# Hybrid decoder layer on one core: gathered operands for the level products, value projection of four heads at once

## The chip, the cores and the metric

The kernel runs on one core of one Trainium2 chip. The metric is the device time of one execution in microseconds (us). "PE" is TensorE, "DVE" VectorE, "ACT" ScalarE, "POOL" GpSimd, "SP" SyncE, which issues most DMAs; "PEld" is TensorE's loading of weights (the stationary operand). A matmul here multiplies a stationary tile of up to 128 x 128 with a moving tile of up to 512 columns into PSUM.

## The reference

One layer over 2048 tokens of width 1024, all in float32. The part that the change touches is the HGRN2 head group (4 heads, key and value width 128):

```python
proj = rmsnorm(h, norm_mix_w) @ w_in          # split into hq, hf, hi, hg and the attention columns
f = lb + (1 - lb) * sigmoid(hf); log_f = log(f); k = 1 - f; q = hq * 128 ** -0.5; v = hi
# per head:  S_t = diag(f_t) S_{t-1} + k_t v_t^T,   o_t = S_t^T q_t
o = rmsnorm(o, hg_norm_w) * silu(hg)
mix = concat([o, sliding_window_attention(...)])  # 8 query heads of 64, window 128, sink logits
h = h + mix @ w_out
h = h + (silu(causal_conv3(v @ w_gate)) * (v @ w_up)) @ w_down   # v = rmsnorm(h); d_ff = 2816
out = rmsnorm(h)
```

Inside a tile of 128 tokens the scores are sums of q_t k_s times the product of the f between s and t. For the kernel's purpose that is a triangle that can be built level by level.

## The kernel before, in words

The sequence is cut into two halves of 1024 tokens (`HALF`), each 8 tiles of 128 (`TT`). Activations lie transposed: features on the partitions, tokens along the free dimension. For each half the program runs a mixing stage (`hgrn`, `attend`, `project_v`), then `out_proj`, `gate_up` and `down`. Projections split each float32 operand into a high and a low part in a matmul format and use three matmuls (high x high, high x low, low x high); a projection of 128 columns is a `unit` of 48 matmuls with 512 moving columns. A weight comes as a 512 KB load into one of 3 `raw` buffers; `prep` (L185) casts its high part on ACT and subtracts it on DVE into one of 2 `hi` and one of 2 `lo` buffers, or, with `slots=True`, into two of the 8 buffers "m" of `slot`. A float32 matmul without such a split is two instructions on PE, and each counts as one in the profile.

Head by head (`HG` = 4) the mixing stage interleaves the generators `hgrn` and `attend`; a scheduler then orders each engine's queue by program order and a simulated timeline, so that independent matmuls (the units q, g, f, hq and, in the last head, `pop` of `out_proj`) are placed between dependent steps. In `hgrn`:

- f and hq are projected (L522, L527); K = 1 - f and Q = q f (L533 to L536) are two tiles with one buffer each.
- the diagonal of the score tile `ST` is a product of K and q (L544).
- seven levels m = 1, 2, 4, ... 64 follow (L590). In a level the tokens form blocks of m; every second block of Q meets the block of K before it. PE writes these products into `plev`. Then every second block of Q (L609) and the other blocks of K (L610) are multiplied with running products F of f, on DVE, in 512 elements each, and F itself is halved (L616, L620). In heads 0 to 2 and m < 32 the K blocks of two tiles are first gathered by ACT into `KK` (L566), so that one stationary tile serves two tiles of tokens (L569, 4 products); the results of the first tile are put into `ST` by a masked copy on DVE (L585), those of the second, which land on the wrong partitions, are copied to `moved` by ACT (L576), shifted by a DMA that ACT's queue issues (`odd`, L579), and placed by a second masked copy one level later (L588). In head 3, which runs beside `out_proj`, there is no gathering: 8 products a level (L602) and one masked copy of 512 elements (L625). m = 32 and m = 64 have 16 and 8 small products (L607), whose results ACT copies (L630).
- K is transposed on PE (`pkn`, L640), multiplied with v (`pu`, L647), and the state is run through the tiles on DVE (`SS`, L651).
- the outputs `po` (L665, L666) are 8 tiles in two PSUM banks; after each tile's products ACT squares them with a sum (L667). rsqrt on DVE, a scaling (`on`, L674), a transpose (`pot`, L679) and a product with the gate (L680) end the head.

`project_v` (L688) computes v for two heads at a time, 8 token tiles x 8 input tiles x 3 matmuls of 256 columns, in heads 0 and 2, with two prepared weights. `BEHIND` (L38) puts pieces of the first `pop` units behind the matmuls of head 3: unit 1 behind level 1, unit 2 in three parts behind `pu`, `po` and `pot`.

```python
elif h % 2 == 0:                                               # L1206
    next(at)
    wv = [prep(a["w_v"][h // 2, s]) for s in range(2)]
    next(hg)
    vs += project_v(hf, wv, X, rs, p)
```

Of the kernel before, what the change touches and what calls it, by code (L numbers as in the profile page):

```python
# [39 lines left out]
NEG = -1.0e30  # L40
UT = 7
RAW = 3
VB = 2
KB = 2
WARM = 12
TAIL_WARM = 7
LV = 4
# [3 lines left out]
def hymba_layer(ctx: ExitStack, tc: tile.TileContext, a: dict, out: bass.AP):  # L51
# [18 lines left out]
    def ps(kind, name):  # L70
        return spaces[kind].tile([P, 512], F32, tag=kind, name=name)
# [448 lines left out]
    def hgrn(hf, h, X, invb, vs, WG, mix, p, fu=None):  # L520
# [13 lines left out]
        nc.vector.tensor_scalar(K, f, -1.0, 1.0, op0=ALU.mult, op1=ALU.add)  # L534
        Q = p.tile([P, HALF], F32, tag="Q", name="Q", bufs=1)
        nc.vector.tensor_tensor(Q, q, f, op=ALU.mult)  # L536


# [19 lines left out]
            yield  # L558

        F, left = f, None  # L560

        def pairs():


            KK = p.tile([P, HALF // 2], F32, tag="KK", name="KK", bufs=KB)
            nc.scalar.copy(KK.rearrange("p (r b c m) -> p r c b m", r=TT // 2, c=2, m=m),  # L566
                           K.rearrange("p (r c b w m) -> p r c b w m", c=2, b=nbc, w=2, m=m)[:, :, :, :, 0])
            for r in range(TT // 2):
                marks[m] = nc.tensor.matmul(pl[:, r * P:(r + 1) * P], KK[:, r * P:(r + 1) * P],  # L569
                                            Qv[:, 2 * r * nbc:2 * (r + 1) * nbc, 1], start=True, stop=True)  # L570

        def place_pairs():

            plv = pl.rearrange("p (r c t) -> p r c t", r=TT // 2, c=2)
            moved, odd = [p.tile([P, TT // 2, 64], F32, tag="lv", name=n, bufs=LV) for n in ("moved", "odd")]
            nc.scalar.copy(moved, plv[:, :, 1])  # L576
# [5 lines left out]
            STv = ST.rearrange("p (r c) (b w m) -> p r c b w m", c=2, w=2, m=m)  # L582
            mk = C.lmask[m].bitcast(U32).rearrange("p (b m) -> p b m", m=m)
            mk = mk.unsqueeze(1).to_broadcast([P, TT // 2, nbc, m])
            nc.vector.copy_predicated(STv[:, :, 0, :, 1], mk, plv[:, :, 0].rearrange("p r (b m) -> p r b m", m=m))  # L585
            r = slice(0, P - m)
            ov = odd[r].rearrange("p r (b m) -> p r b m", m=m)
            return lambda: nc.vector.copy_predicated(STv[r, :, 1, :, 1], mk[r], ov)  # L588

        for m in LEVELS:  # L590
            nb = HALF // (2 * m)
            nbc = 64 // m
            Qv = Q.rearrange("p (b w m) -> p b w m", w=2, m=m)
            Kv = K.rearrange("p (b w m) -> p b w m", w=2, m=m)
# [3 lines left out]
            if paired:  # L598
                pairs()
            elif m < 32:  # L600
                for c in range(TT):
                    marks[m] = nc.tensor.matmul(pl[:, c * 64:(c + 1) * 64], K[:, c * P:(c + 1) * P],  # L602
                                                Qv[:, c * nbc:(c + 1) * nbc, 1], start=True, stop=True)
            else:
                for c in range(TT):
                    for s0 in range(0, P, 2 * m):
                        nc.tensor.matmul(pl[s0:s0 + m, c * m:(c + 1) * m], K[:, c * P + s0:c * P + s0 + m],  # L607
                                         Q[:, c * P + s0 + m:c * P + s0 + 2 * m], start=True, stop=True)
            nc.vector.tensor_tensor(Qv[:, :, 1], Qv[:, :, 1], Fv[:, :, 0:1].to_broadcast([P, nb, m]), op=ALU.mult)  # L609
            done = nc.vector.tensor_tensor(Kv[:, :, 0], Kv[:, :, 0], Fv[:, :, 1:2].to_broadcast([P, nb, m]), op=ALU.mult)  # L610
# [10 lines left out]
            if paired:  # L621
                left = place_pairs()
            elif m < 32:
                mk = C.lmask[m].bitcast(U32).rearrange("p (b m) -> p b m", m=m)
                nc.vector.copy_predicated(ST.rearrange("p c (b w m) -> p c b w m", w=2, m=m)[:, :, :, 1],  # L625
                                          mk.unsqueeze(1).to_broadcast([P, TT, nbc, m]),
                                          pl.rearrange("p (c b m) -> p c b m", c=TT, m=m))
            else:
# [32 lines left out]
        for c in range(TT):  # L661
            cs = slice(c * P, (c + 1) * P)
            prev = state[:, h] if c == 0 else SS[:, c - 1]
            o = po[c // 4][:, c % 4 * P:(c % 4 + 1) * P]
            nc.tensor.matmul(o, ST[:, c], v[:, c], start=True, stop=False)  # L665
            marks["po"] = nc.tensor.matmul(o, Q[:, cs], prev, start=False, stop=True)  # L666
            nc.scalar.activation(on[:, c], o, AF.Square, accum_out=ss[:, c:c + 1])  # L667
        rs = rsqrt(ss, TT, 1.0 / P)
        if h == HG - 1:
            mix[h] = new_x()  # L670
# [16 lines left out]

    def project_v(hf, parts, X, rs, p):  # L688

        v = [p.tile([P, TT, P], F32, tag="v", name="v", bufs=VB) for _ in range(2)]  # L690
        for tt in range(TT):
            o = ps("mm", "pvv")
            t = slice(tt * P, (tt + 1) * P)
            for kt in range(KT):
                hi, lo = parts[kt // 4]
                xh, xl = X[kt]
                c = slice((kt % 4) * 256, (kt % 4 + 1) * 256)
                nc.tensor.matmul(o[:, 0:256], xh[:, t], hi[:, c], start=kt == 0, stop=False)  # L698
                nc.tensor.matmul(o[:, 0:256], xl[:, t], hi[:, c], start=False, stop=False)  # L699
                nc.tensor.matmul(o[:, 0:256], xh[:, t], lo[:, c], start=False, stop=kt == KT - 1)  # L700
            for i in range(2):
                nc.scalar.activation(v[i][:, tt], o[:, i * P:(i + 1) * P], AF.Identity, scale=rs[:, tt:tt + 1])
        return v

    def split_into(h, l, src, eng=None):
        return (nc.scalar.copy(h, src),  # L706
# [480 lines left out]
    for hf in range(NH):  # L1187
        X, kv, invb, rs, f0 = nxt
        with ExitStack() as st:
# [45 lines left out]
def _layout(i):  # L1235
# [17 lines left out]
    w_v = np.stack([cols(w_in, 1024 + pr * 256 + ar(256)).reshape(P, 2, D).transpose(1, 0, 2) for pr in range(2)])  # L1253
    conv = np.concatenate([i["conv_w"][0], i["conv_b"]], 0)
    d = {
        "xT": x.T.reshape(KT, P, S),
# [37 lines left out]
```

## Time and profile before

| what | value |
|---|---|
| time, median of 3 runs | 2198.23 us (2197.66 to 2200.65) |
| span of the profiled execution | 2198.0 us |
| granted TensorE clock | 0.997 |
| PE, DVE, ACT busy | 2180.4, 1639.5, 1049.9 us |
| first half's mixing stage | about 45 to 397 us |
| second half's mixing stage | about 1137 to 1487 us |

The span is that of the first to the last instruction of one execution on the chip, read by its profiler. No other time of that execution is on record; the span lies 0.2 us under the median of the timed runs. A group's row gives line, engine, operation, result<-operands, shapes, count | busy time, mean ns of one | idle time of the engine before it and what ended that. Matmuls overlap in their pipeline, so the time from one start to the next says more than one's duration. Stretches of the first half's mixing stage: head 0 from 45, head 1 from 155, head 2 from 248, head 3 from 342 to 397 us.

### The profile page before, as it was taken

The numbers are of one execution on the slowest core, as the hardware profiler recorded it, in microseconds if no ns is written. First come the engines' busy times: TensorE is split into PE (matmuls) and PEld (weight loads), VectorE is DVE, ScalarE is ACT, GpSimd is POOL, SyncE is SP. The second block draws the span as 40 slices with busy tenths as digits, with TensorE's granted clock in tenths as the row PEclk, the third lists the DMA queues.
The fourth block names the chain that finished last, engine by engine and source line by source line (L and its number), as shares of the span: only waits on it lengthen the run. The fifth ranks groups of instructions, "written<-read, shape, count | busy, mean of one in ns | idle before, by whom it ended". The sixth has DMA issues, their size and how long they took to land.

```text
span 2198.0 us, 29524 instructions
## 1 busy us (share of the span) xinstructions
PE 2180.4 (99%) x11424; PEld 1834.0 (83%) x11424; DVE 1639.5 (75%) x2451; ACT 1049.9 (48%) x1848; POOL 6.3 (0%) x28
## 2 busy tenths in 40 slices
PE   9999999999999999999999999999999999999998
PEld 7988988888888888888889889888888888888888
DVE  6567568688887888885855666677888878887766
ACT  6445544454444445335735455544644444443353
POOL 1000000000000000000000000000000000000000
PEclk9999999999999999999999999999999999999999
DMA  4101112323333234964631111114132323259643
GB/s 155 51 32 48 39 41 68 119 74 102 104 109 108 89 127 143 372 241 156 209 125 41 44 36 51 58 39 134 58 125 92 125 91 109 98 183 393 233 144 130
DMA packets 94358, 257.91 MB, mean 117 GB/s; under 512 B 11594, under 2 KB 17546, under 8 KB 94218
## 3 DMA queue, kind: packets, MB, share of 16 engines
q1 hardware_dynamic: 88992, 251.30, 33.9%
q10 hardware_dynamic: 5226, 4.73, 0.7%
q8 instruction: 89, 1.46, 0.3%
q14 instruction: 51, 0.42, 0.1%
HBM read 195.10 MB, written 57.15 MB: 115 GB/s over the span
## 4 chain that ended last, share of the span: by engine, by line
PE 95%; DVE 3%; ACT 1%; DMA 1%; issue 0%; SPq 0%; DVEq 0%; ACTq 0%
PE X L877 7%; PE X L878 7%; PE X L879 7%; PE pop L212 7%; PE hq L212 4%; PE q L212 4%; PE f L212 4%; PE g L212 4%; PE Y L879 4%; PE Y L878 4%; PE Y L877 4%; PE pdx L1088 3%; PE pdx L1089 3%; PE pdx L1090 3%; PE pdy L1089 3%; PE pdy L1088 3%
## 5 line engine op out<-in xcount | busy, mean ns | idle before, releaser
L706 ACT CAST whi<-raw 128x1024 fp32r<-128x1024 f32 x88 | 92.6, 1053 | 109.2 <-PE X L878 68.2
L877 PE MATMUL X<-T,whi 128*128 128x512 f32 x352 | 136.9, 389 | 0.0
L878 PE MATMUL X<-T,whi 128*128 128x512 f32 x352 | 136.9, 389 | 0.0
L879 PE MATMUL X<-T,wlo 128*128 128x512 f32 x352 | 136.9, 389 | 0.0
L972 DVE SCALAR_TENSOR_TENSOR y<-ga,cw,y 128x1024 f32<-128x1024 f32 x88 | 112.5, 1281 | 26.0 <-ACT y L970 26.0
L884 ACT COPY u<-X 128x512 f32<-128x512 f32 x88 | 51.4, 585 | 133.3 <-PE X L879 133.1
L707 DVE TENSOR_TENSOR wlo<-raw,whi 128x1024 fp32r<-128x1024 f32 x88 | 107.3, 1220 | 0.0
L190 ACT CAST whi<-raw 128x1024 fp32r<-128x1024 f32 x57 | 59.5, 1048 | 93.1 <-PE q L212 31.9
L707 DVE TENSOR_TENSOR xld<-raw,xhd 128x1024 fp32r<-128x1024 f32 x72 | 80.8, 1133 | 19.1 <-ACT xhd L706 18.9
L706 ACT CAST xhd<-raw 128x1024 fp32r<-128x1024 f32 x72 | 69.7, 978 | 43.6 <-DMA raw<-act0T 14.8
L212 PE MATMUL pop<-XL,whi 128*128 128x512 f32 x256 | 86.1, 396 | 2.1 <-DVE XL L224 2.1
L212 PE MATMUL pop<-XH,wlo 128*128 128x512 f32 x256 | 85.2, 393 | 0.8 <-DVE wlo L191 0.8
L212 PE MATMUL pop<-XH,whi 128*128 128x512 f32 x256 | 84.5, 397 | 0.2
L878 PEld LDWEIGHTS X<-T,whi 128*128 128x128 f32 x352 | 66.1, 188 | 13.7
L877 PEld LDWEIGHTS X<-T,whi 128*128 128x128 f32 x352 | 66.1, 188 | 13.7
L879 PEld LDWEIGHTS X<-T,wlo 128*128 128x128 f32 x352 | 66.1, 188 | 13.7
L1088 PE MATMUL pdx<-xhd,hid 128*128 128x512 f32 x192 | 74.4, 391 | 1.0 <-ACT hid L706 1.0
L1089 PE MATMUL pdx<-xld,hid 128*128 128x512 f32 x192 | 74.7, 389 | 0.0
L1090 PE MATMUL pdx<-xhd,lod 128*128 128x512 f32 x192 | 73.7, 389 | 0.0
L698 PE MATMUL pvv<-whi,XH 128*128 128x256 f32 x256 | 73.5, 288 | 0.0
L191 DVE TENSOR_TENSOR wlo<-raw,whi 128x1024 fp32r<-128x1024 f32 x57 | 69.5, 1222 | 4.2 <-ACT whi L190 4.1
L699 PE MATMUL pvv<-whi,XL 128*128 128x256 f32 x256 | 72.6, 284 | 0.0
(379 smaller groups left out, 6563.3 us busy)
## 6 DMA issues: line engine op xcount, KB each, us to landing
wr<-in_w_down SPq DMA_DIRECT2D x90, 512.0 KB, 4.8
raw<-in_w_gate SPq DMA_DIRECT2D x44, 512.0 KB, 3.6
raw<-in_w_up SPq DMA_DIRECT2D x44, 512.0 KB, 3.6
raw<-act0T SPq DMA_DIRECT2D x20, 512.0 KB, 6.1
raw<-act1T SPq DMA_DIRECT2D x20, 512.0 KB, 10.1
act0B<-y SPq DMA_DIRECT2D x33, 256.0 KB, 2.6
act1B<-y SPq DMA_DIRECT2D x33, 256.0 KB, 2.4
raw<-in_w_out SPq DMA_DIRECT2D x16, 512.0 KB, 4.7
```

What stands on the lines that cost most here:

```text
L212: marks["unit"] = nc.tensor.matmul(o[b], w, x[:, bs], start=f, stop=l)
L698: nc.tensor.matmul(o[:, 0:256], xh[:, t], hi[:, c], start=kt == 0, stop=False)
L699: nc.tensor.matmul(o[:, 0:256], xl[:, t], hi[:, c], start=False, stop=False)
L706: return (nc.scalar.copy(h, src), (eng or nc.vector).tensor_tensor(l, src, h.bitcast(F32), op=ALU.subtract))
L707: (eng or nc.vector).tensor_tensor(l, src, h.bitcast(F32), op=ALU.subtract))
L877: nc.tensor.matmul(o, wh[:, ws], xh, start=i == 0 and not more, stop=False, skip_group_check=more)
L878: nc.tensor.matmul(o, wh[:, ws], xl, start=False, stop=False, skip_group_check=more)
L879: r = nc.tensor.matmul(o, wl[:, ws], xh, start=False, stop=i == 3, skip_group_check=more)
L972: nc.vector.scalar_tensor_tensor(y, g[:, w:w + HALF], C.cw[:, ft, w:w + 1], y, op0=ALU.mult, op1=ALU.add)
L1088: nc.tensor.matmul(o, wh[:, i, c], ah[:, i, cols], start=f, stop=False, skip_group_check=more)
L1089: nc.tensor.matmul(o, wh[:, i, c], al[:, i, cols], start=False, stop=False, skip_group_check=more)
L1090: nc.tensor.matmul(o, wl[:, i, c], ah[:, i, cols], start=False, stop=l, skip_group_check=more)
```

## The change

In `hgrn`, Q and K become the two halves of one tile `QK`. Every level, in every head, begins with one copy on ACT that gathers the blocks of both Q and K that the products read into a tile `G` (2 buffers, 1024 elements a partition), pairing tile r with tile r + 4. The products read `G`: 4 products of 128 x 128 for m < 32 in all heads and for m = 64, 16 small ones for m = 32. One DVE multiplication of 1024 elements updates Q and K together, in place of L609 and L610. Head 3 places its results like the others, with `moved`, `odd` and two masked copies of 256 elements. At m = 64 ACT copies the result in two pieces. The squares of `po` are issued behind all 16 products, in a loop of their own. `project_v` runs once in each half, in head 0, for all four heads, with 512 moving columns and four prepared weights, two of them in the slots "m"; one eviction of 512 elements a token tile takes the place of two of 128. Head 2 then takes the path of head 1. The scratch for dynamic DMA descriptors is set to 256.

```diff
-VB = 2
-KB = 2
+GB = 2
@@ hgrn
-        K = p.tile([P, HALF], F32, tag="K", name="K", bufs=1)
+        QK = p.tile([P, 2, HALF], F32, tag="QK", name="QK", bufs=1)
+        Q, K = QK[:, 0], QK[:, 1]
         nc.vector.tensor_scalar(K, f, -1.0, 1.0, op0=ALU.mult, op1=ALU.add)
-        Q = p.tile([P, HALF], F32, tag="Q", name="Q", bufs=1)
         nc.vector.tensor_tensor(Q, q, f, op=ALU.mult)
...
+        R = TT // 2
+        def place(m, pl):
+            plv = pl.rearrange("p (r b c m) -> p r b c m", r=R, c=2, m=m)
+            moved, odd = [p.tile([P, R, 64], F32, tag="lv", name=n, bufs=LV) for n in ("moved", "odd")]
+            nc.scalar.copy(moved.rearrange("p r (b m) -> p r b m", m=m), plv[:, :, :, 1])
             rows_ = P - max(m, 2)
             nc.scalar.dma_start(odd[0:rows_], moved[m:m + rows_])
...
+            nc.vector.copy_predicated(STv[:, 0, :, :, 1], mk, plv[:, :, :, 0])
...
+            return lambda: nc.vector.copy_predicated(STv[r, 1, :, :, 1], mk[r], ov)
         for m in LEVELS:
...
+            part, step = QK.ap[0], QK.ap[-1][0]
+            own = bass.AP(QK.tensor, QK.offset + m * step, [part, [(HALF - m) * step, 2], [2 * m * step, nb], [step, m]])
+            far = bass.AP(QK.tensor, QK.offset + m * step, [part, [(HALF - m) * step, 2], [2 * m * step, nb // 2],
+                                                           [R * P * step, 2], [step, m]])
+            G = p.tile([P, 2, HALF // 2], F32, tag="G", name="G", bufs=GB)
+            nc.scalar.copy(G.rearrange("p t (b c m) -> p t b c m", c=2, m=m), far)
             pl = ps("hg", "plev")
-            paired = m < 32 and h < HG - 1
...
+            if m == 32:
                 for c in range(TT):
+                    for b in range(2):
+                        x = slice(c % R * P + b * 64 + c // R * m, c % R * P + b * 64 + c // R * m + m)
+                        nc.tensor.matmul(pl[2 * b * m:2 * b * m + m, c * m:(c + 1) * m], G[:, 1, x], G[:, 0, x],
+                                         start=True, stop=True)
             else:
...
+                for r in range(R):
+                    x = slice(r * P, (r + 1) * P)
+                    marks[m] = nc.tensor.matmul(pl[:, x], G[:, 1, x], G[:, 0, x], start=True, stop=True)
-            nc.vector.tensor_tensor(Qv[:, :, 1], Qv[:, :, 1], Fv[:, :, 0:1].to_broadcast([P, nb, m]), op=ALU.mult)
-            done = nc.vector.tensor_tensor(Kv[:, :, 0], Kv[:, :, 0], Fv[:, :, 1:2].to_broadcast([P, nb, m]), op=ALU.mult)
+            done = nc.vector.tensor_tensor(own, own, Fv.rearrange("p b w -> p w b").unsqueeze(3).to_broadcast([P, 2, nb, m]),
+                                           op=ALU.mult)
...
+            if m < 32:
+                left = place(m, pl)
+            elif m == 32:
                 for s0 in range(0, P, 2 * m):
                     nc.scalar.copy(ST[s0:s0 + m, :, s0 + m:s0 + 2 * m], ...)
+            else:
+                for c in range(2):
+                    nc.scalar.copy(ST[0:m, c * R:(c + 1) * R, m:],
+                                   pl[c * m:(c + 1) * m].rearrange("p (r c m) -> p r c m", c=2, m=m)[:, :, c])
...
             marks["po"] = nc.tensor.matmul(o, Q[:, cs], prev, start=False, stop=True)
-            nc.scalar.activation(on[:, c], o, AF.Square, accum_out=ss[:, c:c + 1])
+        for c in range(TT):
+            nc.scalar.activation(on[:, c], po[c // 4][:, c % 4 * P:(c % 4 + 1) * P], AF.Square,
+                                 accum_out=ss[:, c:c + 1])
@@ project_v
-        v = [p.tile([P, TT, P], F32, tag="v", name="v", bufs=VB) for _ in range(2)]
+        v = p.tile([P, HG, TT, P], F32, name="v")
...
-                hi, lo = parts[kt // 4]
+                hi, lo = parts[kt // 2]
-                c = slice((kt % 4) * 256, (kt % 4 + 1) * 256)
-                nc.tensor.matmul(o[:, 0:256], xh[:, t], hi[:, c], start=kt == 0, stop=False)
+                c = slice((kt % 2) * 512, (kt % 2 + 1) * 512)
+                nc.tensor.matmul(o, xh[:, t], hi[:, c], start=kt == 0, stop=False)
...
-            for i in range(2):
-                nc.scalar.activation(v[i][:, tt], o[:, i * P:(i + 1) * P], AF.Identity, scale=rs[:, tt:tt + 1])
+            nc.scalar.activation(v[:, :, tt], o.rearrange("p (h d) -> p h d", h=HG), AF.Identity,
+                                 scale=rs[:, tt:tt + 1])
@@ mixing stage
-                elif h % 2 == 0:
+                elif h == 0:
                     next(at)
-                    wv = [prep(a["w_v"][h // 2, s]) for s in range(2)]
+                    wv = [prep(a["w_v"][s], s > 1) for s in range(4)]
                     next(hg)
                     vs += project_v(hf, wv, X, rs, p)
@@ kernel
-    nc = bacc.Bacc("TRN2", target_bir_lowering=False, num_devices=1)
+    nc = bacc.Bacc("TRN2", target_bir_lowering=False, num_devices=1, dynamic_dma_scratch_size=256)
```

More of the change, by code (lines that the diff above doesn't have):

```diff
@@ L560, in hgrn @@
         F, left = f, None
[L562 to L576, printed above, removed]
+        R = TT // 2
[3 more added lines that the diff above has]
+            nc.scalar.copy(moved.rearrange("p r (b m) -> p r b m", m=m), plv[:, :, :, 1])
             rows_ = P - max(m, 2)
@@ L581, in place_pairs @@
                 nc.scalar.dma_start(odd[rows_:rows_ + 1], moved[P - 1:P])
[L582 removed]
+            STv = ST.rearrange("p (c r) (b w m) -> p c r b w m", c=2, w=2, m=m)
             mk = C.lmask[m].bitcast(U32).rearrange("p (b m) -> p b m", m=m)
[L584 to L585 removed]
+            mk = mk.unsqueeze(1).to_broadcast([P, R, 64 // m, m])
+            nc.vector.copy_predicated(STv[:, 0, :, :, 1], mk, plv[:, :, :, 0])
             r = slice(0, P - m)
             ov = odd[r].rearrange("p r (b m) -> p r b m", m=m)
[L588 removed]
+            return lambda: nc.vector.copy_predicated(STv[r, 1, :, :, 1], mk[r], ov)
         for m in LEVELS:
@@ L596, in hgrn @@
+            G = p.tile([P, 2, HALF // 2], F32, tag="G", name="G", bufs=GB)
+            nc.scalar.copy(G.rearrange("p t (b c m) -> p t b c m", c=2, m=m), far)
             pl = ps("hg", "plev")
-            paired = m < 32 and h < HG - 1
-            if paired:
-                pairs()
-            elif m < 32:
+            if m == 32:
                 for c in range(TT):
-                    marks[m] = nc.tensor.matmul(pl[:, c * 64:(c + 1) * 64], K[:, c * P:(c + 1) * P],
-                                                Qv[:, c * nbc:(c + 1) * nbc, 1], start=True, stop=True)
-            else:
[L605 to L608, printed above, removed]
@@ L620, in hgrn @@
                 nc.vector.tensor_tensor(F, Fv[:, :, 0], Fv[:, :, 1], op=ALU.mult)
[L621 to L628, printed above, removed]
+            if m < 32:
+                left = place(m, pl)
+            elif m == 32:
                 for s0 in range(0, P, 2 * m):
@@ L694, in project_v @@
             for kt in range(KT):
-                hi, lo = parts[kt // 4]
+                hi, lo = parts[kt // 2]
                 xh, xl = X[kt]
-                c = slice((kt % 4) * 256, (kt % 4 + 1) * 256)
-                nc.tensor.matmul(o[:, 0:256], xh[:, t], hi[:, c], start=kt == 0, stop=False)
-                nc.tensor.matmul(o[:, 0:256], xl[:, t], hi[:, c], start=False, stop=False)
-                nc.tensor.matmul(o[:, 0:256], xh[:, t], lo[:, c], start=False, stop=kt == KT - 1)
-            for i in range(2):
-                nc.scalar.activation(v[i][:, tt], o[:, i * P:(i + 1) * P], AF.Identity, scale=rs[:, tt:tt + 1])
-        return v
+                c = slice((kt % 2) * 512, (kt % 2 + 1) * 512)
+                nc.tensor.matmul(o, xh[:, t], hi[:, c], start=kt == 0, stop=False)
+                nc.tensor.matmul(o, xl[:, t], hi[:, c], start=False, stop=False)
+                nc.tensor.matmul(o, xh[:, t], lo[:, c], start=False, stop=kt == KT - 1)
+            nc.scalar.activation(v[:, :, tt], o.rearrange("p (h d) -> p h d", h=HG), AF.Identity,
+                                 scale=rs[:, tt:tt + 1])
+        return [v[:, h] for h in range(HG)]
     def split_into(h, l, src, eng=None):
@@ L1252, in _layout @@
     w_out = i["w_out"][0][np.concatenate(rows)]
-    w_v = np.stack([cols(w_in, 1024 + pr * 256 + ar(256)).reshape(P, 2, D).transpose(1, 0, 2) for pr in range(2)])
+    w_v = cols(w_in, 1024 + ar(512)).reshape(P, 4, D).transpose(1, 0, 2)
     conv = np.concatenate([i["conv_w"][0], i["conv_b"]], 0)
```

2 lines of the change are left out of this document (removed).

## The prediction

> **What bounds the kernel now.** I read the page's busy shares first, then the chain that ended last by engine, then the stretches of the mixing stage, then the timeline of PE inside it.
>
> ```profile
> span 2198.0 us, 29524 instructions
> PE 2180.4 (99%) x11424; PEld 1834.0 (83%) x11424; DVE 1639.5 (75%) x2451; ACT 1049.9 (48%) x1848; POOL 6.3 (0%) x28
> PE 95%; DVE 3%; ACT 1%; DMA 1%; issue 0%; SPq 0%; DVEq 0%; ACTq 0%
> ```
>
> PE is busy nearly all the time and 95% of the chain is PE, so in general a PE step saved is time saved, and work added to ACT or DVE is free until PE has to wait for it. That has to be looked at by stage (columns: stretch, length, then busy time and count of PE, PEld, DVE, ACT, POOL):
>
> ```profile
> 155.00:248.00 93.00, 93.00 (x644) 82.16 (x643) 57.77 (x115) 46.67 (x119) 0.00 (x0) 1.00 0.13 38
> 248.00:340.00 92.00, 92.00 (x586) 78.46 (x586) 63.09 (x119) 51.69 (x119) 0.00 (x0) 1.00 0.21 64
> 340.00:397.00 57.00, 54.84 (x410) 46.69 (x408) 43.50 (x91) 21.10 (x71) 0.00 (x0) 0.97 0.10 30
> 344.00:381.00 37.00, 35.31 (x283) 30.06 (x284) 34.07 (x64) 14.52 (x48) 0.00 (x0) 0.95 0.14 44
> ```
>
> Heads 1 and 2 (first two rows) are filled by PE without a gap, with DVE and ACT a third or more idle. Head 3 (third row) is another case: PE has visible idle time (57.00 - 54.84 = 2.2 us a half), and inside it, in the levels (fourth row), DVE is busy 34.07 of 37.00 us. There PE is not alone the bound. The second half's stage is the same work, so I count each term twice.
>
> **Value projection.** Before, 768 matmuls of 256 columns in four blocks; after, 384 of 512. The first rows are from windows that count these matmuls alone (the third sums four windows, both halves); the last three from the chain, whose pieces run from start to start.
>
> ```profile
> 69.96:98.34 28.38, 24.55 (x192) 23.39 (x192) 4.26 (x14) 1.00 0.14 42
> 227.00:257.00 30.00, 25.07 (x192) 23.60 (x192) 4.49 (x14) 1.00 0.08 23
> sum 158.38, PE 99.17 PEld 93.97 ACT 18.58; mean PE 24.79 PEld 23.49 ACT 4.64
> 70.20 0.12 PE pvv L698
> 70.68 0.12 PE pvv L699
> 406.67 52.89 PE pop L212 x232
> ```
>
> A 256-column matmul takes a step of 0.12 us, a 512-column one 52.89 / 232 = 0.228. By steps, 768 x 0.12 - 384 x 0.228 = 92.2 - 87.5 = 4.7 us saved. By the busy sum, which holds the tails where other work cuts in, 99.17 - 87.5 = 11.7. I take 6, near the steps, since the tails partly belong to what cuts in. ACT gets two evictions of 365 ns replaced by one near 721 (rows below): nothing for the path.
>
> A rule of the Trainium skill speaks against this term: the page TensorE: Matmul & The Clock Gate, section Back-to-back issue gap, gives 262 cycles for 256 columns and 518 for 512, so that merging saves 6 cycles a pair, some 1 us in all (an estimate from that page). The trace's 0.12 against half of 0.228 disagrees with it.
>
> **Levels.** PE's timeline, each with the row that starts next:
>
> ```profile
> 161.40 1.07 PE L569 MATMUL plev<-Q,KK 128*128 128x128 f32 x8
> 162.22 0.48 PE L212 MATMUL q<-XH,wlo 128*128 128x512 f32 x1
> 167.57 1.07 PE L569 MATMUL plev<-Q,KK 128*128 128x128 f32 x8
> 200.23 1.15 PE L607 MATMUL plev<-Q,K 128*64 128x64 f32 x16
> 201.30 1.09 PE L495 MATMUL ppt<-ident,sc 128*128 128x128 f32 x8
> 346.72 1.90 PE L602 MATMUL plev<-Q,K 128*128 128x64 f32 x16
> 348.43 0.73 PE L212 MATMUL pop<-XL,whi 128*128 128x512 f32 x2
> ```
>
> A gathered level costs PE 162.22 - 161.40 = 0.82 us, an ungathered one in head 3 348.43 - 346.72 = 1.71. Five levels in two halves: 10 x 0.89 = 8.9 us less. m = 64 goes from 16 small instructions in 201.30 - 200.23 = 1.07 us to 8 large ones like a gathered level, 0.82: 8 heads x 0.25 = 2.0 us less. m = 32 keeps its count and shapes: 0.
>
> What it adds is on ACT and DVE:
>
> ```profile
> L706 ACT CAST whi<-raw 128x1024 fp32r<-128x1024 f32 x88 | 92.6, 1053 | 109.2 <-PE X L878 68.2 <-issue 19.1 <-PE Z L878 13.8
> L975 DVE TENSOR_TENSOR y<-y,invb 128x1024 f32<-128x1024 f32 x44 | 53.8, 1222 | 1.1 <-ACT y L974 1.1
> L609 DVE TENSOR_TENSOR Q<-Q,f 128x512 f32<-128x512 f32 x56 | 38.6, 690 | 30.9 <-PE plev L569 18.6 <-PE plev L607 11.8 <-PE plev L602 0.4
> L566 ACT COPY KK<-K 128x512 f32<-128x512 f32 x30 | 19.1, 636 | 29.6 <-DVE K L610 21.2 <-DVE K L534 8.2
> L702 ACT ACTIVATE v<-pvv,y 128x128 f32<-128x128 f32 x64 | 20.1, 365 | 40.8 <-PE pvv L700 36.5 <-DMA odd<-moved 1.5 <-PE po L665 1.4
> L776 ACT ACTIVATE h<-h,nfw 128x512 f32<-128x512 f32 x28 | 19.6, 721 | 15.7 <-DMA keep<-h 15.7
> ```
>
> ACT: 56 copies of 1024 at 1.05 us in place of 30 of 0.636 is 40 us more, 20 a half, in a stage where its rows above show it idle half the time: 0. If that cover went, it would be 0.4 us a level. DVE: one operation of 1.222 for two of 0.69, 0.16 less each, 9 us in all, hidden except in head 3.
>
> The order of dependences changes more than the work. L609 sat idle 30.9 us behind `plev`: the Q update had to wait until PE had read Q, and each such trip to PE stood behind a run of units. Two levels in head 1 lie 167.57 - 161.40 = 6.2 us apart, of which PE's own part is 0.82. Afterwards only the gathering copy reads QK, so a level's loop is copy plus update, 1.05 + 1.22 = 2.3 us, 3 with handovers, and PE drops out of it; `G` with 2 buffers lets PE lag one level.
>
> Head 3: per half PE saves 5 x 0.89 + 0.25 = 4.7 us, but DVE is nearly full there, and DVE's own sum hardly moves: 7 x 0.16 = 1.1 less for the updates, and for the masked copies these rows (minimum/median/maximum, then the waits of the odd ones):
>
> ```profile
> L585 DVE COPY_PREDICATED ST<-lmask,plev x30: 416/439/753, 75.4 to 1367.0; 128x256 f32<-128x256 uint32 x30
> L625 DVE COPY_PREDICATED ST<-lmask,plev x10: 699/712/1316, 353.2 to 1465.2; 128x512 f32<-128x512 uint32 x10
>   DMA odd<-moved: 18.8, 20
> ```
>
> Two of 439 ns for one of 712 is 0.17 more each. So if DVE sets the pace PE's 4.7 turn into idle time, +9.4 over two halves; if the freed loop removes PE's visible idle time too, -4.3. I take 0, as heads 1 and 2 will also hand over to head 3 earlier. The new shift by DMA adds 10 waits like those 20 (18.8 / 30 = 0.63 us for each of 30 issues, up to 6.3 us); queued behind one on DVE are the next level's F and the softmax steps of `attend`. Most meet a full DVE queue: +2.
>
> **Outputs.** ACT's squares, first and last in head 2, then in head 3, and PE in head 3:
>
> ```profile
> 306.84 0.27 ACT L667 ACTIVATE on<-po 128x128 f32<-128x128 f32 x1
> 329.08 0.27 ACT L667 ACTIVATE on<-po 128x128 f32<-128x128 f32 x1
> 388.31 0.28 ACT L667 ACTIVATE on<-po 128x128 f32<-128x128 f32 x1 [4.92 <-PE po L666]
> 392.27 0.28 ACT L667 ACTIVATE on<-po 128x128 f32<-128x128 f32 x1
> 387.61 0.38 PE L665 MATMUL po<-v,ST 128*128 128x128 f32 x2
> 391.99 0.70 PE L212 MATMUL pop<-XH,whi 128*128 128x512 f32 x2
> 396.18 1.03 PE L679 MATMUL pot<-ident,on 128*128 128x128 f32 x8
> ```
>
> In head 2 the eight squares take 22 us, since products and squares wait for each other in turn and each return finds PE inside a run of units; in head 3, with `pop` held back, 4. With the products in one piece, PE needs 32 x 0.82 / 8 = 3.3 us instead of 391.99 - 387.61 = 4.4: -1.1 a half in head 3, -2.2. But the squares of the second bank then start only when its products end: in head 3 the chain to `pot` grows by between 0.5 us (four squares of 0.4 left) and 1.9 (all eight left), while the `pop` run that covers it (391.99 to 396.18) starts 1.1 earlier. PE idles 1.6 to 3.0 a half; I take 1.8, +3.6. In heads 0 to 2 a unit covers it, and the chain gets some 16 us shorter.
>
> **Loads and order.** Two 512 KB loads and two casts and subtractions (1.05 and 1.22 us) move from head 2 to head 0, on SP's queue past the load of w_g. They use "m" slots, of which 2 of 8 are then in use, and are wanted later than the second of the two weights that already come there. Nothing late: 0. The g unit after the block still waits for a `hi` buffer and 2.3 us of preparation, beside `pu` and scores: between 0 and 2 a half, +1 in all. No DMA is issued by POOL, so the scratch size costs 0.
>
> **Sum:** -6 - 8.9 - 2.0 + 0 + 2 - 2.2 + 3.6 + 1 = -12.5. 2198.0 - 12.5 = 2185.5, and the span lies 0.2 below the median: 2186 (-0.55%).
>
> **Rivals.**
> 1. DVE paces head 3, nothing of PE's saving there stays: +9.4 on the forecast, 2195. For it: 34.07 of 37. Against it: DVE is a third idle in heads 1 and 2, and a shorter chain moves work there.
> 2. PE starves in heads 1 and 2: slower. Their 187 us (155 to 342) lose a projection block of 25 us, so the two heads' chains, now 93 us each, must fit in about 161. Each must shrink by 13 us. If the levels and outputs shrink by less, PE waits: at half of it, 6.5, that is 6.5 x 2 heads x 2 halves = 26 on top, 2212; it turns slower where a chain shrinks by less than 10. Against it: the outputs alone show 22 - 4 = 18 us to be had, the levels 7 x 3.
> 3. All cuts and idle time go as well: 11.7 instead of 6, and -4.3, without the +2, 2174.
> 4. The matmul of 512 columns gains nothing on two of 256 in this place: 2192, less 1 by the skill's rule. The two step rows speak against it.
>
> **How the numbers follow.** Forecast (2178 to 2192) 0.58, rival 1 0.15, rival 2 0.08, rival 3 0.14, rival 4 0.05. 0.2% is 4.4 us, about what a measurement tells from no change: faster means below 2193.8. Rival 1 lies at that edge: 0.05 of it faster, 0.09 same, 0.01 slower. Faster 0.82, same 0.09, slower 0.09. From rival 3 to just past rival 1 the range is 2173 to 2197; rival 2 and half of rival 3's tail stay out.
>
> **What the changed profile would show.** `pvv` with 384 matmuls, steps near 0.228; `plev` with 8 instructions a level in head 3; levels about 3 us apart in head 1; eight squares in a row; head 3 still some 55 us with DVE full, or shorter if rival 3 holds. Wrong would be: idle PE before `plev`, `pdiag` or `po` in heads 1 and 2 (rival 2), an update of much more than 1.22 us or a gathering copy of more than 1.1 through its strides, or waits for `odd` well above 28 us.

## The result and the profile after

| kernel | median (lowest to highest), us | span, us | clock | ratio, 95% interval |
|---|---|---|---|---|
| before, beside it | 2197.94 (2197.41 to 2200.65) | | | 1 |
| changed | 2179.27 (2178.1 to 2180.84) | 2179.1 | 0.998 | 0.9914, 0.99 to 0.9928 |

The change saves 0.86%, 18.7 us. The profiled execution took 2180.84 us, the longest of those timed; its span lies 1.7 us below that time.

The page, the span and the busy shares of the engines:

```profile
span 2179.1 us, 28471 instructions
PE 2159.5 (99%) x10896; PEld 1803.6 (83%) x10896; DVE 1632.4 (75%) x2405; ACT 1091.4 (50%) x1850; POOL 6.0 (0%) x28
```

PE has 11424 - 10896 = 528 instructions less: 384 of the value projection and 144 of the levels. PE is as full as before (99%), and ACT is busy 41.5 us more, near the 40 that were forecast. By stage:

```profile
155.00:248.00 93.00, 93.00 (x601) 78.46 (x597) 65.72 (x120) 50.03 (x111) 0.00 (x0) 1.00 0.14 42
248.00:340.00 92.00, 92.00 (x572) 78.51 (x572) 70.59 (x124) 61.14 (x130) 0.00 (x0) 1.00 0.19 59
340.00:397.00 57.00, 53.69 (x369) 45.24 (x368) 42.77 (x92) 30.74 (x89) 0.00 (x0) 1.00 0.23 76
```

The stretches no longer match the heads. By the starts of `pdiag` and `pot` the chains now run from 175.7 to 232.7, from 244.3 to 306.2 and from 320.8 to 383.2 us: 57 and 62 us for heads 1 and 2, which had 90 and 94. Head 3 takes 62 us where it took 54, and now holds all 48 matmuls of a unit `g` (11.1 us of PE); in the kernel before it held none. PE has still no idle time in the first two rows, although the projection block of head 2 is gone. PE's timeline shows how (one level to the next in head 1; the outputs of head 2, first and last; their squares on ACT, first and last):

```profile
181.83 1.05 PE L600 MATMUL plev<-G 128*128 128x128 f32 x8
184.10 1.05 PE L600 MATMUL plev<-G 128*128 128x128 f32 x8
187.95 1.05 PE L600 MATMUL plev<-G 128*128 128x128 f32 x8
285.03 0.38 PE L656 MATMUL po<-v,ST 128*128 128x128 f32 x2
289.32 0.39 PE L657 MATMUL po<-SS,QK 128*128 128x128 f32 x2
288.01 0.28 ACT L659 ACTIVATE on<-po 128x128 f32<-128x128 f32 x1
290.51 0.29 ACT L659 ACTIVATE on<-po 128x128 f32<-128x128 f32 x1
```

Over this head's seven levels the starts lie 3.1 us apart in the mean, with single steps up to 5.2, where they lay 6.5 apart. The output products of head 2 take 4.4 us in this half and 10.6 in the second, where they took 20.5 and 21.0. The two operations that make a level's loop, and the shift by DMA:

```profile
L589 ACT COPY G<-QK 128x1024 f32<-128x1024 f32 x56 | 63.7, 1138 | 53.5 <-DVE QK L535 25.2 <-DVE QK L601 24.5 <-DVE ST L575 1.8
L601 DVE TENSOR_TENSOR QK<-QK,f 128x1024 f32<-128x1024 f32 x56 | 68.7, 1226 | 5.2 <-ACT G L589 4.8
  DMA odd<-moved: 10.7, 14
```

And the value projection, one step to the next, and its 192 matmuls of a half in one window:

```profile
70.77 0.39 PE L693 MATMUL pvv<-wlo,XH 128*128 128x512 f32 x1
71.00 0.39 PE L691 MATMUL pvv<-whi,XH 128*128 128x512 f32 x1
69.00:125.00 56.00, 45.63 (x192) 35.47 (x192) 5.50 (x8) 1.00 0.19 59
```

What is new on PE is one wait, twice, in head 3 (chain of waits: engine, what waited, for what; us, times, longest):

```profile
PE pkn L631 <- ACT ST L621: 4.5, 2, 2.4
```

**Where the 18.9 us of span went.** I add PE's time by tile, from one matmul's start to the next, over the whole span: `pvv` 94.5 to 88.9 (-5.6), `plev` 55.7 to 44.4 (-11.3), `pop` 182.4 to 175.9 (-6.5), `pkn` 8.0 to 11.9 (+3.9); the rest adds up to 0.6 us. A second sum is used below for every kernel. Each matmul is priced at its undisturbed step (0.227 us with 512 columns, 0.12 with 256, with 128 or fewer by the load of its stationary tile: 0.112 for 128 columns of it, 0.058 for 64, 0.025 for 32; `pinv`, a float32 product that isn't split, has 0.43 at 512 columns); what the trace has beyond that is called stall (waits, changes between kinds of matmul, half clock). Steps: 2150.6 before, 2136.4 after, so -5.0 by the projection and -9.2 by the levels. Stall: 39.9 before, 35.3 after, of which head 3, from its first `pdiag` to its last `pot` in both halves, has 14.5 and 12.3. So 14.2 of the 18.9 us are steps.

### The profile page after: what moved, and what is told of

Its sections match the earlier page's. It is cut to its first block, busy times and chain, and to the rows that moved or that the text cites. A ratio compares the mean times of both kernels' runs of the same rounds, so it can differ in the third digit from the quotient of the medians.

```text
span 2179.1 us, 28471 instructions
## 1 busy us (share of the span) xinstructions
PE 2159.5 (99%) x10896; PEld 1803.6 (83%) x10896; DVE 1632.4 (75%) x2405; ACT 1091.4 (50%) x1850; POOL 6.0 (0%) x28
## 5 line engine op out<-in xcount | busy, mean ns | idle before, releaser
L700 DVE TENSOR_TENSOR xld<-raw,xhd 128x1024 fp32r<-128x1024 f32 x72 | 80.7, 1132 | 20.5 <-ACT xhd L699 20.2
L589 ACT COPY G<-QK 128x1024 f32<-128x1024 f32 x56 | 63.7, 1138 | 53.5 <-DVE QK L535 25.2
L601 DVE TENSOR_TENSOR QK<-QK,f 128x1024 f32<-128x1024 f32 x56 | 68.7, 1226 | 5.2 <-ACT G L589 4.8
```

Of the source, the lines that this page charges most:

```text
L601: done = nc.vector.tensor_tensor(own, own, Fv.rearrange("p b w -> p w b").unsqueeze(3).to_broadcast([P, 2, nb, m]), op=ALU.mult)
L700: (eng or nc.vector).tensor_tensor(l, src, h.bitcast(F32), op=ALU.subtract))
```

## Experiments

The change has three parts: levels (L), squares behind the products (S), merged projection (P). All eight combinations ran, and five variants in size or place beside them. The scratch size was not varied by itself. Each ratio is to the kernel before on the same chip. Its interval is some 0.0012 to each side, 2.7 us, so a difference of two rows is uncertain by about 4 us. The steps and the stall are those of the profiled execution, which can lie off the median: for S it is 3.6 us below, for S and L 3.5 below, for the changed kernel 1.6 above.

| parts | ratio, 95% interval | in us of 2198 | steps | stall |
|---|---|---|---|---|
| none (before) | 1 | 0 | 2150.6 | 39.9 |
| P | 1.0166, 1.0152 to 1.018 | +36.5 | 2145.6 | 81.0 |
| S | 1.0021, 1.0012 to 1.003 | +4.6 | 2150.6 | 40.1 |
| L | 0.9968, 0.9956 to 0.9981 | -7.0 | 2141.4 | 42.7 |
| P and S | 0.9976, 0.9966 to 0.9985 | -5.3 | 2145.6 | 38.3 |
| P and L | 0.997, 0.9959 to 0.9982 | -6.6 | 2136.4 | 47.1 |
| S and L | 0.9939, 0.9926 to 0.9951 | -13.4 | 2141.4 | 32.1 |
| all (changed) | 0.9914, 0.99 to 0.9928 | -18.9 | 2136.4 | 35.3 |

**Merged projection alone.** The kernel before with `project_v`, its dispatch and the scratch size of the changed one:

```diff
-                elif h % 2 == 0:
+                elif h == 0:
                     next(at)
-                    wv = [prep(a["w_v"][h // 2, s]) for s in range(2)]
+                    wv = [prep(a["w_v"][s], s > 1) for s in range(4)]
```

> The kernel before with the merged value projection alone (four heads in head 0, 512 columns, the scratch size); levels and squares as before. Theory A (the time is the sum of PE's steps): from the two traces the projection's starts add up to 94.5 us before and 88.9 after, so 2198 - 5.6 = about 2192. Theory B (head 1 and 2 need the projection as cover for their chains of 93 us each, and only the shorter chains of the levels and squares set it free): each half loses 25 us of cover, so slower, between 2205 and 2240, with idle PE in heads 1 and 2.

Measured 2235.92 us, ratio 1.0166 (1.0152 to 1.018). The two stretches that were heads 2 and 3 before, and PE's longest waits:

```profile
248.00:340.00 92.00, 88.03 (x541) 74.44 (x540) 64.94 (x124) 52.68 (x118) 0.00 (x0) 0.98 0.17 51
340.00:397.00 57.00, 44.56 (x341) 39.62 (x340) 40.16 (x81) 20.11 (x68) 0.00 (x0) 0.86 0.13 42
PE ppt L495 <- DVE sc L486: 6.7, 2, 5.5
PE ppt L495 <- DVE y L176: 6.4, 1, 6.4
PE poT L506 <- DVE pp L498: 4.5, 2, 3.5
PE plev L602 <- DVE K L610: 3.7, 3, 1.5
```

This is the prediction's rival 2: 5 us of steps saved, 41 us of stall added. The chains of heads 1 and 2 run from 175.9 to 274 and from 276.8 to 357, 98 and 80 us where they were 90 and 94, so no shorter in sum by more than 6, with 25 us of cover taken away; PE waits for DVE at the steps of levels and of `attend`, and between 340 and 397 us, the end of head 2 and most of head 3, it is idle 12.4 of 57 us.

**Merged projection undone.** The changed kernel with two blocks of 256 columns again.

```diff
-                elif h == 0:
+                elif h % 2 == 0:
                     next(at)
-                    wv = [prep(a["w_v"][s], s > 1) for s in range(4)]
+                    wv = [prep(a["w_v"][h // 2, s]) for s in range(2)]
```

> The changed kernel with the projection put back into two blocks of 256 columns in heads 0 and 2; gathered levels and squares stay. Theory A: 2179.1 + 5.6 = about 2185, levels and squares alone are worth 13. Theory B says the same for this kernel, or a little less if the levels' gain was stall and not steps: 2183 to 2186. If the levels' gain depends on where the projection stands, it is above 2188.

Measured 2186.19 us, ratio 0.9939 (0.9926 to 0.9951): the projection is worth (0.9939 - 0.9914) x 2198 = 5.5 us in the changed kernel, uncertain by about 4, beside 5.0 of steps. It can't tell the theories apart, as both said.

**Squares in the loop again.**

```diff
             marks["po"] = nc.tensor.matmul(o, Q[:, cs], prev, start=False, stop=True)
-        for c in range(TT):
-            nc.scalar.activation(on[:, c], po[c // 4][...], AF.Square, accum_out=ss[:, c:c + 1])
+            nc.scalar.activation(on[:, c], o, AF.Square, accum_out=ss[:, c:c + 1])
```

> The changed kernel with each square issued right behind its tile's products again. Theory A: PE's steps are the same but for head 3, where the outputs took 4.4 us with the squares between and 3.6 behind: +0.8 a half, about 2181. The prediction's step (squares behind the products lengthen the chain in head 3 and cost 3.6 us, gain 2.2): 2178. Theory B (the chain of heads 1 and 2 gets 18 us longer a head and PE runs out of cover): 2185 or more, idle PE in heads 1 and 2.

Measured 2192.07 us, ratio 0.997 (0.9959 to 0.9982). PE's steps are the changed kernel's to the instruction; the stall is 11.8 us more, nearly all of it in head 3 (22.9 against 12.3):

```profile
340.00:397.00 57.00, 51.08 (x352) 43.27 (x352) 42.84 (x88) 28.70 (x81) 0.00 (x0) 0.97 0.16 44
PE plev L600 <- ACT G L589: 3.6, 3, 2.2
PE pop L211 <- DVE XL L223: 2.9, 2, 2.3
PE poT L505 <- DVE pp L497: 2.5, 2, 1.3
308.09 0.28 ACT L658 ACTIVATE on<-po 128x128 f32<-128x128 f32 x1 [5.13 <-PE po L657]
308.54 0.28 ACT L658 ACTIVATE on<-po 128x128 f32<-128x128 f32 x1
315.37 0.28 ACT L658 ACTIVATE on<-po 128x128 f32<-128x128 f32 x1
```

The last three rows are squares of head 2: in pairs some 6 to 7 us apart, a unit of projection between them. Its outputs take 25 us (301.9 to 327.0) instead of 4.4, and head 3's `pdiag` starts at 338.9 instead of 320.8 us, so that a unit that would have covered head 3 is used up before it. The matmuls of `g` inside the first half's head 3, in the changed kernel and here:

```profile
320.80:383.30 62.50, 11.14 (x48) 8.94 (x48) 2.62 (x4) 1.19 (x2) 1.00 0.25 78
338.90:392.30 53.40, 0.00 (x0) 0.00 (x0) 2.75 (x4) 1.20 (x2) 0.97 0.15 42
```

**Head 3 ungathered.** For m < 32, head 3 reads Q and K as before, with 8 products a level and one masked copy of 512 elements.

```diff
+            alone = h == HG - 1 and m < 32
-            G = p.tile([P, 2, HALF // 2], F32, tag="G", name="G", bufs=GB)
-            nc.scalar.copy(G.rearrange("p t (b c m) -> p t b c m", c=2, m=m), far)
+            if not alone:
+                G = p.tile([P, 2, HALF // 2], F32, tag="G", name="G", bufs=GB)
+                nc.scalar.copy(G.rearrange("p t (b c m) -> p t b c m", c=2, m=m), far)
...
+                    marks[m] = nc.tensor.matmul(pl[:, c * 64:(c + 1) * 64], K[:, c * P:(c + 1) * P],
+                                                Qv[:, c * nbc:(c + 1) * nbc, 1], start=True, stop=True)
```

> The changed kernel with head 3 at m < 32 as before: eight products a level straight from K and Q, one masked copy of 512, no shift by DMA; the joint update stays. Theory A: 10 levels x 0.89 us of PE come back, 2188. Rival (DVE paces head 3, so PE's saving there was idle time): less than 3 us, 2179 to 2182. Theory B adds to A that the update waits for PE again in head 3: above 2190.

Measured 2194.24 us, ratio 0.9983 (0.9974 to 0.9992), 15 us above the changed kernel. Steps are 2145.4, 9.0 more; stall 39.6, 4.3 more. This is theory B: the update waits for PE again, six times and 12.0 us in sum; no such wait is listed for the changed kernel.

```profile
DVE QK L608 <- PE plev L596: 12.0, 6, 3.0
```

So none of PE's saving in head 3 had turned into idle time: rival 1 of the prediction falls. That DVE was busy 34.07 of 37 us there did not make it the pace.

**One gather buffer.**

```diff
-GB = 2
+GB = 1
```

> The changed kernel with one buffer G instead of two: the next level's gathering copy must wait until PE has read the last one, so each level again makes a trip through PE's queue; PE's instructions are the same. Theory A (sum of steps): 2179 to 2180. Theory B (what sets PE free is that PE is out of the levels' loop): levels in heads 1 and 2 about 6 us apart again instead of 2.3 to 5, and more idle PE late in the mixing stage: 2185 to 2200.

Measured 2198.91 us, ratio 1.0001 (0.9993 to 1.001): with the same instructions on PE and one buffer the change is worth nothing, as its theory B said. Three levels of head 1, head 3, and the largest wait:

```profile
182.05 1.05 PE L600 MATMUL plev<-G 128*128 128x128 f32 x8
188.85 1.05 PE L600 MATMUL plev<-G 128*128 128x128 f32 x8
195.25 1.05 PE L600 MATMUL plev<-G 128*128 128x128 f32 x8
340.00:397.00 57.00, 50.29 (x345) 41.76 (x345) 41.21 (x88) 26.71 (x83) 0.00 (x0) 0.94 0.13 40
PE plev L600 <- ACT G L589: 6.1, 4, 3.2
```

6.8 and 6.4 us between levels, as before the change: with one buffer a copy waits until PE has read the last one, and PE reads when it comes out of a run of a unit. The stall is 54.0, and 27.7 of it lie in head 3, which starts at 339.6 us and has no `g` matmul left. It is not the gathering that shortens the chain but that PE may lag a level behind.

**Level 64 copied by DVE in head 3.** Meant to remove the new wait of `pkn`: ACT's two copies of the level's result stand behind eight exponentials, and `pkn`, which takes its PSUM from the same pool as the level, waits for them. PE and ACT at the first of the two waits, in the changed kernel:

```profile
360.98 0.39 ACT L480 ACTIVATE sc<-sc,m 128x128 f32<-128x128 f32 x1
361.49 0.37 ACT L466 COPY sc<-psc 128x256 f32<-128x256 f32 x1
361.75 0.74 ACT L621 COPY ST<-plev 64x256 f32<-64x256 f32 x2
362.55 0.66 PE L631 MATMUL pkn<-ident,QK 128*128 128x128 f32 x4 [2.08 <-ACT ST L621]
```

```diff
-                    nc.scalar.copy(ST[0:m, c * R:(c + 1) * R, m:],
+                    (nc.vector.tensor_copy if h == HG - 1 else nc.scalar.copy)(
+                                   ST[0:m, c * R:(c + 1) * R, m:],
```

> The changed kernel, but in head 3 the two copies of the m = 64 result run on DVE instead of ACT, where they stand behind eight exponentials while PE waits with the transposes of K (2.2 and 2.6 us). If that wait is all: 2179 - 4.9 = about 2174. If the next thing in the chain is late by as much (the scores' exponentials, which the products of attend wait for): 2178 to 2180.

Measured 2182.26 us, ratio 0.9926 (0.9913 to 0.9938): no gain, as its rival said, and a little above the 2178 to 2180 that it gave. The wait of `pkn` is gone, and these came:

```profile
PE ppt L494 <- DVE sc L485: 3.1, 1, 3.1
PE pu L639 <- ACT Kn L633: 2.5, 1, 2.5
```

**Squares alone**, in the kernel before (the same loop as in the changed kernel).

```diff
-            nc.scalar.activation(on[:, c], o, AF.Square, accum_out=ss[:, c:c + 1])
+        for c in range(TT):
+            nc.scalar.activation(on[:, c], po[c // 4][...], AF.Square, accum_out=ss[:, c:c + 1])
```

> The kernel before with only the squares moved behind the products. Theory A: PE saves the pauses between the output products in head 3, 0.8 a half: 2196.6. The prediction's step (cost 3.6, gain 2.2 in head 3): 2199.6. Theory B: chains are 16 us shorter but cover was enough, so nothing in heads 1 and 2: as A.

Measured 2203.59 us, ratio 1.0021 (1.0012 to 1.003): slower by 4.6 us, a miss of the theory by which they gain, and also more than the 1.4 us net that the prediction charged. Head 3 starts 18 us earlier (324.6 against 342.8), but its `pot` comes at 397 us as before. So here, where heads 1 and 2 had cover enough, shortening their chains gains nothing and only moves the cover. Why it loses 4.6 us isn't settled: the profiled execution is the shortest of eleven, 3.6 us under their median, and its stall (40.1) is that of before.

**Projection and squares** together, in the kernel before, with both edits above.

> The kernel before with the merged projection and the squares moved, levels as before. The prediction put the point where starvation turns it slower at 10 us a chain; the squares alone shorten a chain by 16 to 18. If that account by chain length holds, the kernel is not slower than 2198 (2192 to 2198). If the place of the cover counts, not only its sum (the levels still make a trip through PE each): 2200 to 2225.

Measured 2192.65 us, ratio 0.9976 (0.9966 to 0.9985). The squares turn the merged projection's +36.5 into -5.3. This is the account by chain length. Stall is 38.3, against 81.0 without them; between 340 and 397 us PE is idle for 3 us instead of 12:

```profile
340.00:397.00 57.00, 53.94 (x403) 45.50 (x403) 42.41 (x86) 18.43 (x59) 0.00 (x0) 1.00 0.07 20
```

**Levels alone**: the changed kernel with the projection in two blocks and the squares between the products.

> The changed kernel with two parts undone: the value projection in two blocks of 256 columns again and each square again right behind its product. What is left of the change is the gathering of Q and K in all heads. Theory A (the parts add up): the PE steps that the levels alone save are 2150.6 - 2141.4 = 9.2 us (the two sums of steps of the kernel before and of the changed one with its projection undone), the stalls stay at 40: about 2189 us. Theory B (a part that makes the chains shorter is only worth what PE is short of; with the projection undone heads 1 and 2 have 25 us more of cover a half, so squares between products cost little here, less than the 13 us that they cost in the changed kernel): 2187 to 2192 us. Rival C (squares cost the same 13 us with any cover): 2186 + 13 = 2199 us, no gain over before.

Measured 2191.7 us, ratio 0.9968 (0.9956 to 0.9981). Rival C falls: squares between products cost (0.9968 - 0.9939) x 2198 = 6.4 us here and 12.3 where the projection is merged. A and B can't be told apart by this number. Here head 3 keeps the 48 matmuls of `g`, with the squares between the products or behind them, so a used-up unit isn't the whole price of the squares.

**Three gather buffers.**

```diff
-GB = 2
+GB = 3
```

> The changed kernel with three buffers for the gathered copies (GB = 3 in place of 2). Theory A (the second buffer took PE out of the loop of a level; from there the loop is copy plus update, 1.14 + 1.23 us, which a third buffer doesn't shorten): no change against the changed kernel, 2177 to 2181 us. Rival (copies still wait for PE to have read the buffer two levels back, where PE stands inside a run of a unit of some 5 us or more): some 5 us faster, 2174 us.

Measured 2179.47 us, ratio 0.9912 (0.9898 to 0.9926): no change, as theory A said. Its reason isn't shown: copy and update make 2.3 us, but the copies of head 1 start 2.4 to 5.3 us apart with two buffers and 2.5 to 5.3 with three. The third buffer does bring the last copy forward, from 23.6 us behind the first to 20.8; what the run shows is that a chain shorter than that of the changed kernel is worth nothing here.

**Unit 1 of the output projection in three parts** in head 3:

```diff
-BEHIND = {1: {0: 1}, 2: {0: "pu", 2: "po", 5: "pot"}}
+BEHIND = {1: {0: 1, 3: 16, 5: 64}, 2: {0: "pu", 2: "po", 5: "pot"}}
```

> The changed kernel, and unit 1 of the output projection in head 3 held back in three parts: 3 of its 8 steps behind level 1 as before, 2 behind level 16, 3 behind level 64 (1.37 us of PE each), in place of all 8 behind level 1. Theory A (the new wait of PE for the copies of level 64, 2.25 and 2.6 us, is short of cover alone): 4.1 us of matmuls stand there, the wait goes and the half clock behind it too, 5 us faster, 2174 us. Rival (cover is only moved: the levels between 1 and 16 then lack it, 4 levels at 2.4 us of copy and update against 4 x 0.8 of PE plus three steps of the unit): PE waits for G instead, same or slower, 2179 to 2186 us.

Measured 2179.74 us, ratio 0.9911 (0.9897 to 0.9924): nothing gained, and the wait stays. The matmuls that were held back run directly behind level 64 and are through when PE comes to the second four transposes, which still wait:

```profile
PE pkn L631 <- ACT ST L621: 4.1, 2, 2.1
```

None of the variants beats the changed kernel by more than its interval.

## Why the prediction was right, and where its sizes were off

Direction and mechanism held: 2179.27 lies inside 2173 to 2197, at a gain of 18.7 us where 12 were forecast. The two large terms, projection and levels, came out in sum as forecast. The rest was summed to a loss and came out as a gain, and the part that made the difference had no price in the sum; that the range held all the same was partly luck. Term by term:

- **Value projection, -6**: -5.6 in the trace, 5.0 by steps, 5.5 by the experiment. The step of 0.227 us against two of 0.12 is as the rows said; rival 4 falls. The "two evictions of 365 ns replaced by one near 721" are four over both blocks of a half (64 rows before, 16 after); one takes 5.50 / 8 = 0.69, so ACT saves 9 us (20.1 to 11.0), off the path.
- **Levels, -8.9, and m = 64, -2.0**: `plev` has 11.3 us less in the trace. Head 3's ten levels with m < 32 take 8.3 us where they took 17.6, so 9.4; put back, they make the kernel 15 us slower. The eight levels with m = 64 take 6.9 us in sum where they took 8.5, so 1.7: four of the eight have the 0.82 of the forecast, the others 0.9.
- **Update and copy**: forecast 1.222 and 1.05; 1.226 and 1.138 in the mean. That mean is over the bound of 1.1 that was set for "wrong", but the strides cost only in the smallest blocks. The median of the 56 copies is 1.054; the eight with m = 1 take 1.50 to 1.55 us, the eight with m = 2 take 1.18 to 1.22, and all with m = 4 or more 1.05 to 1.06. The first three of head 1:

```profile
174.30 1.52 ACT L589 COPY G<-QK 128x1024 f32<-128x1024 f32 x1 [2.72 <-DVE QK L535]
179.57 1.18 ACT L589 COPY G<-QK 128x1024 f32<-128x1024 f32 x1 [3.75 <-DVE QK L601]
183.19 1.06 ACT L589 COPY G<-QK 128x1024 f32<-128x1024 f32 x1
```

- **Head 3 gives nothing back, 0**: PE's idle time inside the first half's head 3 is 3.3 us where it was 2.2, and its stall in the two halves 12.3 where it was 14.5. The head did not stay "some 55 us": with the unit `g` in it, it takes 62. Waits of `pop` went, the one of `pkn` (4.5 us) came. That wait, behind ACT's exponentials, is not in the prediction.
- **Waits for `odd`, +2**: the step "the new shift by DMA adds 10 waits like those 20" failed. 40 levels have 14 such waits of 10.7 us in sum, where 30 levels had 20 of 18.8. Whether they cost PE anything isn't shown; in the second half's head 3 the chain that ended last goes through two of these shifts before it reaches the exponentials and `pkn`:

```profile
1420.15 6.75 DMA odd<-moved
1426.96 3.40 DMA odd<-moved
```

- **Squares, -2.2 and +3.6**: this is the term that was sized most wrongly. The gain in head 3 is there: its products take 3.59 us from their first start to what starts next, where they took 4.38, so -1.6 in the two halves. The cost isn't: no wait of PE for squares, for `on` or in `pot` is among its longest in the changed kernel. The larger mistake was to look only at head 3, and to write of heads 0 to 2 "a unit covers it, and the chain gets some 16 us shorter" without a price. Putting the squares back costs 12.3 us in the changed kernel, where head 3 loses its unit `g`, and 6.4 with the projection in two blocks, where it keeps it (each uncertain by about 4); in the kernel before, where cover wasn't short, moving them gained nothing.
- **g preparation, +1**: no wait of PE for it is listed.

The four cost terms summed to +4.4 (2 + 3.6 - 2.2 + 1) and came out as about -2 (-18.9 of span, less the -5.6 and -11.3). That is the 6.4 us between forecast and result.

**Rival 2** was the closest call. Its condition is that each chain must shrink by about 13 us when the projection block leaves head 2. The chains of heads 1 and 2 in the first half, and what the merged projection is worth with them:

| kernel | chains, us | against before, us | stall |
|---|---|---|---|
| before | 90 and 94 | 0 | 39.9 |
| P | 98 and 80 | +36.5 | 81.0 |
| P and L | 74 and 84 | -6.6 | 47.1 |
| P and S | 81 and 80 | -5.3 | 38.3 |
| all (changed) | 57 and 62 | -18.9 | 35.3 |

With 6 us shrunk in sum PE starves. With 23 (P and S), near the 25 that the block took, it doesn't; with 26 (P and L) it stalls 7 us more than before, so length alone doesn't settle it. By the rival's rule, four times what each chain lacks to 13, P should stall some 40 us more, and it did by 41. Levels or squares alone bring P from 36.5 us slower to 5 or 7 faster than before; but beside the levels alone P is worth nothing (-6.6, and -7.0 without it). The mechanism that the prediction held against itself is real, and the chain had to be shortened for the forecast to hold. Chains also hold whatever PE runs between their steps, so their length is a measure of cover left as much as of dependences.

## What to carry to other kernels

Where one engine is full, independent work is the cover of dependent chains, and taking it away (a merged block, a block moved forward) costs what the chain can't give up, here 41 us of stall for 5 us of steps: compare the chain's length with the work left beside it before pricing the step saved. A reordering that shortens a chain has no price of its own; moving the squares was worth +4.6 us alone, -12.3 in the full change and -41.8 beside the merged projection without the levels, so such a term belongs to the combination. A copy that lets the full engine lag needs the buffer to lag into: one buffer less, and all 19 us were gone.

## What the runs showed of the hardware

The granted clock of PE falls to half for short stretches. In the clock records of the traces each stretch inside the span is 3.41 us long or a whole multiple of it, and within a trace they start whole multiples of 3.41 us apart. By these steps, around the wait of the second half and that of the first half in the changed kernel, then in the kernel before (the columns behind the length are PE's busy time and count; the one behind POOL is the clock):

```profile
1440.01:1443.42 3.41, 1.16 (x9) 0.71 (x7) 0.81 (x4) 3.34 (x15) 0.00 (x0) 1.00 0.02 5
1443.43:1446.84 3.41, 3.21 (x15) 2.98 (x16) 3.38 (x5) 1.60 (x4) 0.00 (x0) 0.50 0.00 0
...
357.99:361.40 3.41, 2.48 (x21) 2.20 (x20) 0.49 (x3) 3.38 (x17) 0.00 (x0) 1.00 0.02 5
361.40:364.81 3.41, 2.03 (x16) 1.79 (x17) 3.25 (x6) 2.41 (x7) 0.00 (x0) 1.00 0.00 0
...
364.85:368.26 3.41, 2.73 (x25) 2.26 (x24) 3.41 (x8) 0.00 (x0) 0.00 (x0) 1.00 0.00 0
368.26:371.67 3.41, 3.41 (x28) 2.75 (x25) 2.62 (x6) 0.28 (x1) 0.00 (x0) 0.50 0.00 0
```

So a wait can be paid a second time: 3.41 us at half clock are 1.7 us of PE's work lost, behind a wait of 2.4. Between 340 and 397 us of the merged projection alone the clock is 0.86, 8 us on top of 12.4 idle. The two waits of the changed kernel differ in place too: the second half's 2.4 us lie in one step, the first half's 2.08 are split over two, and no stretch follows them. Over all thirteen traces, 19 of the 21 full-clock steps in which PE was busy for less than half are followed by the half clock, and 6 of the 18 in which it was busy for 0.5 to 0.6 (the last steps of a span left out). But 9 stretches follow busier steps: the one of the kernel before above, and 8 at the start of the second half, where PE runs 17 to 24 `pst` products of one moving column. So PE's busy time alone doesn't decide, and what does was not tried. The Trainium skill's page TensorE: Matmul & The Clock Gate, section What's actually happening, has the half rate follow an idle window of about 3.4 us; the rows show it behind steps of 3.41 us in which PE was busy for 1.16 and for 2.73 of them.
